# Gates spread by one product in the rounded format instead of one in full fp32

## The chip, the cores and the metric

The kernel runs on one core of a Trainium2 chip. The metric is the device time of one execution in microseconds; the median of the runs is compared. Five engines share the work: TensorE (PE; PEld its weight loads), VectorE (DVE), ScalarE (ACT), GpSimd (POOL) and SyncE (SP), each with an in-order queue of its own. Beside them the DMA engines move data.

## The reference, cut to what matters

Two transformer blocks run over 256 tokens of width 2048. The edit lies in the last part of the second one, a layer that picks 128 of 16384 experts for each token (8 heads, 16 each) and weighs them by a gate:

```
def peer_ffn(h, w_pq, sub_keys, u_tab, v_tab):
    ...
    expert = (e1 * N_KEYS + e2).reshape(T, PEER_HEADS * PEER_TOPK)
    gate = jax.nn.softmax(best, axis=-1).reshape(T, PEER_HEADS * PEER_TOPK).astype(h.dtype)
    ...
        u = jnp.take(u_tab, ec, axis=0)
        act = jax.nn.gelu(jnp.einsum('cd,ckd->ck', hc, u), approximate=False) * gc
        vv = jnp.take(v_tab, ec, axis=0)
        return jnp.einsum('ck,ckd->cd', act, vv)
```

An expert's number is e1 * 128 + e2, with e1 and e2 from 0 to 127.

## The kernel before

The kernel gathers no rows of `u_tab`. In `_peer` it computes Gelu(h u) for all 16384 experts and all 256 tokens, and multiplies the result by a matrix of gates that is zero where an expert wasn't picked. The result is `S_`, two tiles in SBUF: `sa` for the values 0 to 51 of e2 (SA = 52) and `sb` for 52 to 127, with e1 on the partitions and the tokens innermost. The next stage multiplies `S_` by `v_tab`.

The loop over i (64 passes) computes two values of e2 each. `_proj` streams 16 chunks of `u` through `_stream`: a DMA into `raw`, a ScalarE copy into the rounded format (`hi`, float32r, L252), a VectorE subtraction for the rest (`lo`, L255), 512 elements each, and per 128 columns three TensorE products of 256 moving columns (hi by hh, hi by hl, lo by hh) into `acc`. So each pass has 8 `hi`, 8 `lo` and 96 products. `hi` and `lo` have four buffers each. VectorE then scales `acc` into `gtmp` (L1564), ScalarE applies Gelu in one or two pieces (L1565, L1568), and `keep` sends the result to DRAM (`wide`) by DMAs that ScalarE issues (L1498). GpSimd multiplies the tokens whose gates are already there (L1570).

From i = G0 = 27 to 60 the loop also spreads gates, 256 tokens over 34 passes. `spread(g, e)` does four tokens (L1516 to L1539). For each token t the 128 picks lie on the partitions: `sel[:, 0]` is e1, `sel[:, 1]` is e2, `sel[:, 2]` the gate. A one-hot `oh1` (128 picks by 128 values of e1) and a one-hot `oh2` times the gate (128 picks by 128 values of e2) are built from `iota`, and one product of the two in full fp32 gives the token's matrix of gates in PSUM (`ps_g`). `oh1` is built in turn by VectorE and GpSimd (L1528), `oh2` by VectorE (L1529). For the e2 that are already computed, up to e, VectorE multiplies `S_` by `ps_g` (L1537); into the rest, where nothing stands yet, ScalarE copies `ps_g` (L1539).

The order of each engine's queue is set when the kernel is built: a scheduler interleaves the instructions of passes and spreads by its own cost model, and the queues then run strictly in that order, with semaphores between the engines. Pools limit how far ahead an engine may be: `gq` three buffers of one-hots (two tokens each), `psw` four banks for `ps_g`, `g1` one `gtmp`.

Of the kernel before, what the change touches and what calls it, by code (L numbers as in the profile page):

```python
# [10 lines left out]
F32 = mybir.dt.float32  # L11
# [1473 lines left out]
def _peer(k, I, O, hctx, pers, sa, tctx, t1, x3n, wide, rb):  # L1485
# [21 lines left out]
    with ExitStack() as sctx:  # L1507
        with ExitStack() as c:
            k.acc = c.enter_context(tc.tile_pool(name="accp", bufs=3, space=bass.MemoryType.PSUM, side="right"))
            k.psw = c.enter_context(tc.tile_pool(name="pswp", bufs=4, space=bass.MemoryType.PSUM))  # L1510
            t2 = tctx.enter_context(tc.tile_pool(name="rt2", bufs=2))
            route = _Route(k, I, rb, t1, t2)
            gq = None
            done = 0

            def spread(g, e):  # L1516


                ps = k.psw.tile([128, 4, 128], F32, name="ps_g", tag="psw")
                i0 = None  # L1520
                for j in range(4):
                    t = g * 4 + j
                    if j % 2 == 0:
                        a = gq.tile([128, 2, 128], F32, name="oh1")
                        b = gq.tile([128, 2, 128], F32, name="oh2")
                    aj, bj = a[:, j % 2], b[:, j % 2]
                    eng = nc.gpsimd if j % 2 else nc.vector
                    eng.tensor_scalar(aj, iota, sel[:, 0, t:t + 1], None, op0=OP.is_equal)  # L1528
                    nc.vector.tensor_scalar(bj, iota, sel[:, 1, t:t + 1], sel[:, 2, t:t + 1], op0=OP.is_equal, op1=OP.mult)  # L1529
                    i = _mm(k, ps[:, j], aj, bj, start=j == 0, stop=True)  # L1530
                    if j == 0:
                        i0 = i
                    else:
                        _after(k, i, i0)
                for s_, lo, hi in parts(0, e):
                    s_ = s_[:, :, g * 4:g * 4 + 4]
                    nc.vector.tensor_tensor(s_, s_, ps[:, :, lo:hi].rearrange("p t e -> p e t"), op=OP.mult)  # L1537
                for s_, lo, hi in parts(e, 128):
                    nc.scalar.activation(s_[:, :, g * 4:g * 4 + 4], ps[:, :, lo:hi].rearrange("p t e -> p e t"), AF.Copy)  # L1539


            for i in range(64):
                if i % 3 == 0 and i < 24:
                    route.head(i // 3)
                if i == 24:
                    route.finish(sel, picks)
                if i == SA // 2:
                    tctx.close()
                    sp = sctx.enter_context(tc.tile_pool(name="sb", bufs=1))
                    S_[1] = sp.tile([128, 128 - SA, 256], F32, name="sb")  # L1550
                    gq = c.enter_context(tc.tile_pool(name="gq", bufs=3))
                    g1 = c.enter_context(tc.tile_pool(name="gq1", bufs=1))
                    iota = g1.tile([128, 128], F32, name="iota")
                    nc.scalar.dma_start(iota, _cst(I, "iota"))
                ps = k.acc.tile([128, 2, 256], F32, name="acc")
                _proj(k, ps, I["u"][i], (0, KT), k.hh, k.hl)
                dst = next(parts(2 * i, 2 * i + 2))[0]
                if done == 0:
                    nc.vector.tensor_tensor(dst, ps, _bc2(rb), op=OP.mult)
                    nc.scalar.activation(dst, dst, AF.Gelu)  # L1560
                    keep(dst, i, 0, 256)
                else:
                    tmp = g1.tile([128, 2, 256], F32, name="gtmp")
                    nc.vector.tensor_tensor(tmp, ps, _bc2(rb), op=OP.mult)  # L1564
                    nc.scalar.activation(tmp[:, :, :done], tmp[:, :, :done], AF.Gelu)  # L1565
                    keep(tmp, i, 0, done)
                    if done < 256:
                        nc.scalar.activation(dst[:, :, done:], tmp[:, :, done:], AF.Gelu)  # L1568
                        keep(dst, i, done, 256)
                    nc.gpsimd.tensor_tensor(dst[:, :, :done], dst[:, :, :done], tmp[:, :, :done], op=OP.mult)  # L1570
                if i >= G0:
                    while done < 256 and done * (G1 - G0) < 256 * (i + 1 - G0):
                        spread(done // 4, 2 * i + 2)
                        done += 4
        hctx.close()

        with ExitStack() as c:
            pso = c.enter_context(tc.tile_pool(name="pso", bufs=1, space=bass.MemoryType.PSUM))
            v2 = c.enter_context(tc.tile_pool(name="v2", bufs=4, side="right"))
            k.raw2 = c.enter_context(tc.tile_pool(name="raw2", bufs=5, side="right"))  # L1580
            out = [[pso.tile([128, 512], F32, name=f"o{t}{q}") for q in range(4)] for t in range(2)]
            rows = c.enter_context(tc.tile_pool(name="vr", bufs=RB, side="right"))
            sums = _row_sums(k, picks, wide, rows, [out[t][3] for t in range(2)])
            taken = 0
            k.own, split = None, []

            def halves(e):


                src = S_[0][:, e] if e < SA else S_[1][:, e - SA]  # L1590
                ah = v2.tile([128, 256], F32R, name="ah")
                al = v2.tile([128, 256], F32R, name="al")
                nc.scalar.activation(ah, src, AF.Copy)
                i = nc.gpsimd.tensor_tensor(al, src, ah.bitcast(F32), op=OP.subtract)
                if k.own is not None:
                    k.tc.add_manual_dep(i.ins, k.own.ins.name, SYNC, reason="beside the sums")
                split.append((ah, al))

            halves(0)
            halves(1)  # L1600
            for e in range(128):
                ah, al = split.pop(0)
                for g, (vh, vl, _) in enumerate(_stream(k, I["v"][e], D - DS)):
                    for t in range(2):
                        ts = slice(t * 128, t * 128 + 128)
                        for n, (s_, m_) in enumerate(((ah, vh), (ah, vl), (al, vh))):
                            _mm(k, out[t][g], s_[:, ts], m_, start=e == 0 and n == 0, stop=e == 127 and n == 2)
                if e == 24:

                    xn = [S_[0][:, 8 * t:8 * t + 8].rearrange("p a b -> p (a b)").rearrange("p (a b) -> p a b", b=512) for t in range(2)]  # L1610
                    for t in range(2):
                        nc.scalar.dma_start(xn[t], x3n[t].rearrange("p (a b) -> p a b", b=512))
                while taken < 128 and taken * 122 < (e - 2) * 128:
                    next(sums, None)
                    taken += 1
                if e < 126:
                    halves(e + 2)
            for _ in sums:
                pass
            k.raw2 = None  # L1620
            sctx.close()
            fin = c.enter_context(tc.tile_pool(name="fin", bufs=1))
            nf = fin.tile([128, 4, 512], F32, name="nf")
            nc.scalar.dma_start(nf.rearrange("p a b -> p (a b)"), I["normf"].to_broadcast([128, D]))
            for t in range(2):
                ss = fin.tile([128, 4], F32, name=f"ss{t}")
                sq = fin.tile([128, 512], F32, name=f"fsq{t}")
                for q in range(4):
                    nc.vector.tensor_tensor(xn[t][:, q], xn[t][:, q], out[t][q], op=OP.add)
                    nc.scalar.activation(sq, xn[t][:, q], AF.Square, accum_out=ss[:, q:q + 1])  # L1630
                v = fin.tile([128, 1], F32, name=f"fv{t}")
                nc.vector.tensor_reduce(v, ss, axis=AX.X, op=OP.add)
                nc.vector.tensor_scalar(v, v, 1.0 / D, EPS, op0=OP.mult, op1=OP.add)
                r = _rsqrt(k, fin, v, 1, f"f{t}")
                for q in range(4):
                    nc.vector.scalar_tensor_tensor(xn[t][:, q], xn[t][:, q], r, nf[:, q], op0=OP.mult, op1=OP.mult)
                    (nc.sync if q % 2 else nc.scalar).dma_start(O["out"][t * 128:t * 128 + 128, q * 512:q * 512 + 512], xn[t][:, q])
# [146 lines left out]
```

## Time and profile before

| | |
|---|---|
| median of 3 runs | 3341.68 us (3337.93 to 3341.87) |
| profiled execution | 3346.09 us, span 3344.3 us |
| PE busy | 3243.8 us (97%) |
| PEld busy | 3051.6 us (91%) |
| DVE busy | 2480.0 us (74%) |
| ACT busy | 1570.2 us (47%) |
| POOL busy | 833.5 us (25%) |
| `ps_g` products | 512 instructions, from 2257.5 to 2737.5 us of the span |

The shares are averages over the whole span; for one stage a window has to be cut out. The chain of work that ended last is 86% TensorE. Busy time of an engine that isn't the bound costs nothing by itself; what counts is the wait that ends last.

### The profile page before, as it was taken

To read this page: it belongs to the slowest core of one execution; us is meant where nothing else is said; L and a number is where in the kernel's file an instruction comes from. 1 tells how busy PE (TensorE), PEld (TensorE's weight loads), DVE (VectorE), ACT (ScalarE), POOL (GpSimd) and SP (SyncE) were. 2 spreads that over 40 slices of the span, in tenths; PEclk is the share of its full clock that TensorE was granted. 3 is DMA by queue.
4 is the path that set the end of the run, shared out by engine and by line. 5 is a ranking of instruction groups with operands and counts; after the bars stand their busy time and mean duration, and the time that the engine had idled before them with its cause. 6 is when DMAs were issued, how large, how long until landed. Compare 5 with 4: busy or idle time off the path is not lost.

```text
span 3344.3 us, 65878 instructions
## 1 busy us (share of the span) xinstructions
PE 3243.8 (97%) x25018; PEld 3051.6 (91%) x25018; DVE 2480.0 (74%) x5503; ACT 1570.2 (47%) x2810; POOL 833.5 (25%) x1010
## 2 busy tenths in 40 slices
PE   8999899999999989999999899999999999999998
PEld 8999899999999979888869899999999997777776
DVE  8775587777754468887865687786777777999898
ACT  5444454444433345554454544444444444455554
POOL 3110100000000044444510000001222326666663
PEclk9999999999999989999999999999999999999999
DMA  5545455555555556444228766666656669999996
GB/s 196 162 160 171 145 169 180 188 179 188 179 187 183 180 178 208 151 132 137 91 88 261 242 208 193 203 187 196 180 174 182 180 185 319 355 347 345 345 344 237
DMA packets 240366, 680.47 MB, mean 203 GB/s; under 512 B 59184, under 2 KB 89776, under 8 KB 215856
## 3 DMA queue, kind: packets, MB, share of 16 engines
q1 hardware_dynamic: 168848, 560.53, 51.8%
q0 software_dynamic: 20480, 83.90, 7.1%
q10 hardware_dynamic: 50720, 31.82, 3.2%
q8 instruction: 196, 3.21, 0.4%
q14 instruction: 122, 1.00, 0.1%
HBM read 649.55 MB, written 60.16 MB: 212 GB/s over the span
## 4 chain that ended last, share of the span: by engine, by line
PE 86%; DVE 5%; DMA 4%; issue 2%; ACT 2%; POOL 1%; ACTq 0%; SPq 0%; DVEq 0%; POOLq 0%
PE acc L260 59%; PE o L260 15%; PE held L260 3%; PE ps_g L260 2%; PE R L260 1%; DMA raw<-in_w_out 1%; DVE lo L255 1%; ACT hi L252 1%; PE ps_S L260 1%; PE ps_p L260 1%; DMA x3n<-nat 0%; DVE hl L350 0%; PE ps_sc L260 0%; PE ps_m L260 0%; PE ps_go L260 0%
## 5 line engine op out<-in xcount | busy, mean ns | idle before, releaser
L252 ACT ACTIVATE hi<-raw 128x512 fp32r<-128x512 f32 (+1 forms) x1582 | 1146.4, 732 | 1335.3 <-PE acc L260 838.3
L255 DVE TENSOR_TENSOR lo<-raw,hi 128x512 fp32r<-128x512 f32 (+1 forms) x1492 | 1224.7, 835 | 631.3 <-ACT hi L252 588.1
L260 PE MATMUL acc<-hh,hi 128*128 128x256 f32 x4928 | 1403.5, 285 | 14.1 <-ACT hh L349 12.4
L260 PE MATMUL acc<-hh,lo 128*128 128x256 f32 x4928 | 1404.5, 286 | 9.9 <-DVE lo L255 9.1
L260 PE MATMUL acc<-hl,hi 128*128 128x256 f32 x4928 | 1398.1, 284 | 6.9 <-DVE hl L350 6.8
L260 PEld LDWEIGHTS acc<-hh,hi 128*128 128x128 f32 x4928 | 935.3, 190 | 17.6 <-ACT hh L349 13.2
L260 PEld LDWEIGHTS acc<-hl,hi 128*128 128x128 f32 x4928 | 935.4, 190 | 10.2 <-DVE hl L350 9.1
L260 PEld LDWEIGHTS acc<-hh,lo 128*128 128x128 f32 x4928 | 929.4, 189 | 15.1 <-DVE lo L255 12.0
L260 PE MATMUL o<-lo,ah 128*128 128x512 f32 x768 | 305.2, 398 | 2.5 <-issue 2.5
L260 PE MATMUL o<-hi,al 128*128 128x512 f32 x768 | 304.6, 397 | 0.9 <-issue 0.9
L1456 POOL DMA_INDIRECT vrow<-wide,prow x256 | 264.5, 1033 | 68.5 <-issue 42.7
L260 PE MATMUL o<-hi,ah 128*128 128x512 f32 x768 | 222.5, 399 | 8.5 <-ACT hi L252 5.8
L260 PE MATMUL acc<-gh,lo 128*128 128x256 f32 x704 | 199.2, 283 | 0.0
L260 PE MATMUL acc<-gl,hi 128*128 128x256 f32 x704 | 199.2, 283 | 0.0
L260 PE MATMUL acc<-gh,hi 128*128 128x256 f32 x704 | 199.2, 283 | 0.0
L260 PEld LDWEIGHTS o<-hi,ah 128*128 128x128 f32 x768 | 143.4, 189 | 48.7 <-ACT hi L252 10.7
L1528 POOL TENSOR_SCALAR oh<-iota,sel 128x128 f32<-128x128 f32 x128 | 95.4, 756 | 351.1 <-PE ps_g L260 321.1
L260 PEld LDWEIGHTS o<-lo,ah 128*128 128x128 f32 x768 | 145.0, 189 | 38.5 <-issue 2.9
L1478 DVE SCALAR_TENSOR_TENSOR o<-vrow,pval,o 128x512 f32<-128x512 f32 x254 | 179.1, 750 | 0.0
L260 PEld LDWEIGHTS o<-hi,al 128*128 128x128 f32 x768 | 145.0, 189 | 36.6 <-issue 1.3
L255 POOL TENSOR_TENSOR lo<-raw,hi 128x512 fp32r<-128x512 f32 (+1 forms) x90 | 135.1, 1503 | 170.4 <-ACT hi L252 154.3
L699 POOL MEMSET u<- 128x4 f32 x44 | 4.5, 103 | 653.7 <-DVE y L707 510.6
(474 smaller groups left out, 4366.8 us busy)
## 6 DMA issues: line engine op xcount, KB each, us to landing
raw<-in_u SPq DMA_DIRECT2D x256, 512.0 KB
raw<-in_w_up SPq DMA_DIRECT2D x85, 1024.0 KB
raw<-in_v SPq DMA_DIRECT2D x128, 512.0 KB
raw<-in_w_in SPq DMA_DIRECT2D x43, 1024.0 KB
raw<-in_w_dn SPq DMA_DIRECT2D x40, 1024.0 KB
wide<-in_vs SPq DMA_DIRECT2D x128, 256.0 KB
raw<-in_v SPq DMA_DIRECT2D x128, 256.0 KB
raw<-in_w_rkv SPq DMA_DIRECT2D x48, 512.0 KB
```

Of the source, the lines that this page charges most:

```text
L252: nc.scalar.activation(hi[:, :m], raw[:, a:a + m], AF.Copy)
L255: k.low = eng.tensor_tensor(lo[:, :m], raw[:, a:a + m], hi[:, :m].bitcast(F32), op=OP.subtract)
L260: return k.nc.tensor.matmul(out, lhsT, rhs, start=start, stop=stop, skip_group_check=True)
L699: nc.gpsimd.memset(u[:, :, 0:2], 0.0)
L1456: nc.gpsimd.indirect_dma_start(r, None, wide, bass.IndirectOffsetOnAxis(ap=picks.row[:, t, j:j + 1], axis=0), element_offset=128 * t)
L1478: i = nc.vector.scalar_tensor_tensor(acc[t], v, w, acc[t], op0=OP.mult, op1=OP.add)
L1528: eng.tensor_scalar(aj, iota, sel[:, 0, t:t + 1], None, op0=OP.is_equal)
```

## The change

`spread` now does two tokens instead of four. The gate is split once into a rounded part (`gate`, float32r) and the rest (written back into `sel[:, 2]`). For each token, `oh2` has two halves of 128 columns side by side, one times each part, all one-hots are in the rounded format, and one product of 256 moving columns gives both halves in PSUM. They have to be added afterwards: ScalarE copies the first half, VectorE adds the second. For the e2 already computed the sum goes into a new tile `gsum` (one for `sa`, one for `sb`) and VectorE multiplies `S_` by it in a further instruction; for the rest it goes straight into `S_`. GpSimd builds both `oh1` of a pair and one of the four halves of `oh2`; VectorE builds the other three. The pool `gq` has two buffers instead of three.

```diff
             def spread(g, e):
...
-                ps = k.psw.tile([128, 4, 128], F32, name="ps_g", tag="psw")
+                ps = k.psw.tile([128, 2, 2, 128], F32, name="ps_g", tag="psw")
+                a = gq.tile([128, 2, 128], F32R, name="oh1")
+                b = gq.tile([128, 2, 2, 128], F32R, name="oh2")
                 i0 = None
-                for j in range(4):
-                    t = g * 4 + j
-                    if j % 2 == 0:
-                        a = gq.tile([128, 2, 128], F32, name="oh1")
-                        b = gq.tile([128, 2, 128], F32, name="oh2")
-                    aj, bj = a[:, j % 2], b[:, j % 2]
-                    eng = nc.gpsimd if j % 2 else nc.vector
-                    eng.tensor_scalar(aj, iota, sel[:, 0, t:t + 1], None, op0=OP.is_equal)
-                    nc.vector.tensor_scalar(bj, iota, sel[:, 1, t:t + 1], sel[:, 2, t:t + 1], op0=OP.is_equal, op1=OP.mult)
-                    i = _mm(k, ps[:, j], aj, bj, start=j == 0, stop=True)
+                for j in range(2):
+                    t = g * 2 + j
+                    nc.gpsimd.tensor_scalar(a[:, j], iota, sel[:, 0, t:t + 1], None, op0=OP.is_equal)
+                    for n, w in enumerate((gate, sel[:, 2])):
+                        eng = nc.gpsimd if n and j else nc.vector
+                        eng.tensor_scalar(b[:, j, n], iota, sel[:, 1, t:t + 1], w[:, t:t + 1], op0=OP.is_equal, op1=OP.mult)
+                    i = _mm(k, ps[:, j].rearrange("p n e -> p (n e)"), a[:, j], b[:, j].rearrange("p n e -> p (n e)"),
+                            start=j == 0, stop=True)
...
-                for s_, lo, hi in parts(0, e):
-                    s_ = s_[:, :, g * 4:g * 4 + 4]
-                    nc.vector.tensor_tensor(s_, s_, ps[:, :, lo:hi].rearrange("p t e -> p e t"), op=OP.mult)
-                for s_, lo, hi in parts(e, 128):
-                    nc.scalar.activation(s_[:, :, g * 4:g * 4 + 4], ps[:, :, lo:hi].rearrange("p t e -> p e t"), AF.Copy)
+                for (s_, lo, hi), past in [(x, True) for x in parts(0, e)] + [(x, False) for x in parts(e, 128)]:
+                    s_ = s_[:, :, g * 2:g * 2 + 2]
+                    h, l = (ps[:, :, n, lo:hi].rearrange("p t e -> p e t") for n in range(2))
+                    if past:
+                        to = gq.tile([128, 128, 2], F32, name="gsum")[:, :hi - lo]
+                    else:
+                        to = s_
+                    nc.scalar.activation(to, h, AF.Copy)
+                    nc.vector.tensor_tensor(to, l, to, op=OP.add)
+                    if past:
+                        nc.vector.tensor_tensor(s_, s_, to, op=OP.mult)
...
-                    gq = c.enter_context(tc.tile_pool(name="gq", bufs=3))
+                    gq = c.enter_context(tc.tile_pool(name="gq", bufs=2))
...
+                    gate = g1.tile([128, 256], F32, name="gate")
+                    nc.scalar.activation(gate.bitcast(F32R), sel[:, 2], AF.Copy)
+                    nc.vector.tensor_tensor(sel[:, 2], sel[:, 2], gate, op=OP.subtract)
```

Because the scheduler lays the queues out anew, the order around the edit changes too. First ScalarE, around the two Gelus of one pass in the middle of the stage, before. A name's number is its buffer; what stands in brackets is what the instruction waits for.

```order
L252 ACTIVATE hi_29961<-raw_29959 128x512 [waits DMAHW4_49,DVE_49,PE_49]
L252 ACTIVATE hi_29977<-raw_29959 128x512 [waits DVE_49,PE_49]
L1565 ACTIVATE gtmp_29876<-gtmp_29876 128x2x76 [waits DMAHW0_49,DVE_49]
L1568 ACTIVATE sb_27763<-gtmp_29876 128x2x180
L1498 DMA wide_13452<-gtmp_29876 128x2x76 [waits Activation_49]
L1498 DMA wide_13452<-sb_27763 128x2x52 [waits Activation_49]
L1498 DMA wide_13452<-sb_27763 128x2x128 [waits DMAHW1_49]
L252 ACTIVATE hi_29995<-raw_29993 128x512 [waits DMAHW5_49,PE_49]
L252 ACTIVATE hi_30011<-raw_29993 128x512 [waits PE_49]
L1539 ACTIVATE sb_27763<-ps_g_29884 128x52x4 [waits DVE_49]
```

The same place after, at a pass a little later in the stage (L1574 and L1577 are the Gelus, L1542 the copies out of PSUM):

```order
L1542 ACTIVATE gsum_30982<-ps_g_30971 128x104 [waits DVE_49]
L1542 ACTIVATE sb_27763<-ps_g_30805 128x48x2 [waits DVE_49]
L252 ACTIVATE hi_31126<-raw_31124 128x512 [waits DMAHW2_49,PE_49,Activation_49]
L1574 ACTIVATE gtmp_30963<-gtmp_30963 128x2x98 [waits DMAHW5_49,DVE_49,Pool_49]
L1577 ACTIVATE sb_27763<-gtmp_30963 128x2x158
L1498 DMA wide_13452<-gtmp_30963 128x2x98 [waits Activation_49]
L1498 DMA wide_13452<-sb_27763 128x2x30 [waits DMAHW6_49,Activation_49]
L1498 DMA wide_13452<-sb_27763 128x2x128
L1542 ACTIVATE gsum_30986<-ps_g_30971 128x60 [waits DVE_49]
L1542 ACTIVATE gsum_31003<-ps_g_30992 128x104 [waits DVE_49]
L252 ACTIVATE hi_31142<-raw_31124 128x512 [waits PE_49]
```

Copies that wait for VectorE now stand both ahead of the Gelus and right behind the three DMA issues, ahead of the next `hi`.

VectorE, from `gtmp` of a pass on, before (L1537 multiplies `S_` by `ps_g`):

```order
L1564 TENSOR_TENSOR gtmp_29876<-acc_29739,rs_bcp_22242 128x512 [waits DMAHW0_49,PE_49,Pool_49]
L1537 TENSOR_TENSOR sa_20991<-sa_20991,ps_g_29884 128x52x4 [waits PE_49]
L1528 TENSOR_SCALAR oh1_30070<-iota_27770,sel_22346 128x128
L1529 TENSOR_SCALAR oh2_30071<-iota_27770,sel_22346 128x128 x2
L255 TENSOR_TENSOR lo_29978<-raw_29959,hi_29977 128x512 [waits Activation_49]
L1528 TENSOR_SCALAR oh1_30078<-iota_27770,sel_22346 128x128 [waits PE_49]
L1529 TENSOR_SCALAR oh2_30079<-iota_27770,sel_22346 128x128 x2
L1537 TENSOR_TENSOR sa_20991<-sa_20991,ps_g_29904 128x52x4 [waits PE_49]
```

And after, from `gtmp` of the pass shown above on (L1543 adds, L1545 multiplies):

```order
L1573 TENSOR_TENSOR gtmp_30963<-acc_30826,rs_bcp_22242 128x512 [waits DMAHW5_49,PE_49]
L255 TENSOR_TENSOR lo_31109<-raw_31090,hi_31108 128x512 [waits Activation_49]
L1545 TENSOR_TENSOR sb_27763<-sb_27763,gsum_30820 128x28x2 [waits DVE_49]
L1543 TENSOR_TENSOR gsum_30982<-ps_g_30971,gsum_30982 128x104 [waits Activation_49]
L1543 TENSOR_TENSOR sb_27763<-ps_g_30805,sb_27763 128x48x2 [waits Activation_49]
L255 TENSOR_TENSOR lo_31127<-raw_31124,hi_31126 128x512 [waits DMAHW2_49,PE_49,Activation_49]
L1545 TENSOR_TENSOR sa_20991<-sa_20991,gsum_30982 128x52x2 [waits DVE_49]
...
L1543 TENSOR_TENSOR gsum_30986<-ps_g_30971,gsum_30986 128x60 [waits Activation_49]
L1543 TENSOR_TENSOR gsum_31003<-ps_g_30992,gsum_31003 128x104 [waits Activation_49]
L1545 TENSOR_TENSOR sa_20991<-sa_20991,gsum_31003 128x52x2 [waits DVE_49]
L255 TENSOR_TENSOR lo_31143<-raw_31124,hi_31142 128x512 [waits PE_49,Activation_49]
```

Three two-operation one-hots stand where the row of dots is. Each multiplication waited for TensorE before; each addition waits for ScalarE now.

## Rows read from the trace of the kernel before

**Rows 1.** Busy time of each engine from 2350 to 2700 us, clock, DMA share.

```profile
core 0: us, PE busy (x) PEld busy (x) DVE busy (x) ACT busy (x) POOL busy (x), PEclk, DMA share, GB/s
2350.00:2700.00 350.00, 348.74 (x2936) 348.36 (x2935) 266.37 (x637) 161.51 (x314) 98.20 (x129) 1.00 0.61 180
```

**Rows 2.** Who waited for whom, same stretch: us in total, times, longest.

```profile
DVE lo L255 <- ACT hi L252: 59.8, 84, 1.5
...
PE acc L260 <- DVE lo L255: 1.3, 2, 0.9
```

**Rows 3.** TensorE in order of time: start us, us, instruction, count.

```profile
2506.77 0.28 PE L260 MATMUL acc<-hh,hi 128*128 128x256 f32 x1
2506.89 0.28 PE L260 MATMUL acc<-hl,hi 128*128 128x256 f32 x1
2507.00 1.05 PE L260 MATMUL ps_g<-oh,oh 128*128 128x128 f32 x8
2507.81 0.37 PE L260 MATMUL acc<-hh,lo 128*128 128x256 f32 x1
```

**Rows 4.** VectorE in order of time over one pass of the loop.

```profile
2551.99 0.69 DVE L1564 TENSOR_TENSOR gtmp<-acc,rs_bcp 128x512 f32<-128x512 f32 x1 [0.26 <-PE acc L260]
2552.60 0.30 DVE L1528 TENSOR_SCALAR oh<-iota,sel 128x128 f32<-128x128 f32 x1
2552.80 0.71 DVE L1529 TENSOR_SCALAR oh<-iota,sel 128x128 f32<-128x128 f32 x2
2553.42 0.68 DVE L255 TENSOR_TENSOR lo<-raw,hi 128x512 fp32r<-128x512 f32 x1
2554.03 0.36 DVE L1537 TENSOR_TENSOR sa<-sa,ps_g 128x208 f32<-128x208 f32 x1
2554.31 0.28 DVE L1528 TENSOR_SCALAR oh<-iota,sel 128x128 f32<-128x128 f32 x1
2554.50 1.10 DVE L1529 TENSOR_SCALAR oh<-iota,sel 128x128 f32<-128x128 f32 x2
...
2555.72 0.59 DVE L1529 TENSOR_SCALAR oh<-iota,sel 128x128 f32<-128x128 f32 x2
2556.24 0.36 DVE L1537 TENSOR_TENSOR sa<-sa,ps_g 128x208 f32<-128x208 f32 x1
...
2565.29 0.69 DVE L1564 TENSOR_TENSOR gtmp<-acc,rs_bcp 128x512 f32<-128x512 f32 x1 [0.26 <-PE acc L260]
```

**Rows 5.** ScalarE and its issues (ACTq) in order of time, two passes.

```profile
2552.72 0.45 ACT L1565 ACTIVATE gtmp<-gtmp 128x288 f32<-128x288 f32 x1 [0.27 <-DVE gtmp L1564]
...
2555.04 0.48 ACTq L1498 DMA_DIRECT2D wide<-sb  x1
2555.62 1.26 ACT L252 ACTIVATE hi<-raw 128x512 fp32r<-128x512 f32 x2 [2.18 <-PE acc L260]
...
2566.01 0.46 ACT L1565 ACTIVATE gtmp<-gtmp 128x304 f32<-128x304 f32 x1 [0.27 <-DVE gtmp L1564]
...
2567.43 0.70 ACTq L1498 DMA_DIRECT2D wide<-sb  x1
```

**Rows 6.** GpSimd: its one-hots as a group, then in order of time.

```profile
L1528 POOL TENSOR_SCALAR oh<-iota,sel 128x128 f32<-128x128 f32 x102 | 75.5, 751 | 251.5 <-PE ps_g L260 228.0 <-DVE lo L255 11.7 <-DVE sb L1537 9.1
...
2665.45 1.62 POOL L1528 TENSOR_SCALAR oh<-iota,sel 128x128 f32<-128x128 f32 x1 [4.20 <-PE ps_g L260]
2671.41 1.81 POOL L1528 TENSOR_SCALAR oh<-iota,sel 128x128 f32<-128x128 f32 x3 [4.34 <-PE ps_g L260]
2673.19 1.30 POOL L1570 TENSOR_TENSOR sb<-sb,gtmp 128x424 f32<-128x424 f32 x1
```

**Rows 7.** VectorE in order of time beside these GpSimd instructions.

```profile
2665.39 1.98 DVE L255 TENSOR_TENSOR lo<-raw,hi 128x512 fp32r<-128x512 f32 x3
...
2672.75 0.78 DVE L255 TENSOR_TENSOR lo<-raw,hi 128x512 fp32r<-128x512 f32 x1
2673.45 1.12 DVE L1529 TENSOR_SCALAR oh<-iota,sel 128x128 f32<-128x128 f32 x1
```

**Rows 8.** A ScalarE copy out of PSUM, by form, 2550 to 2600 us.

```profile
L1539 ACT ACTIVATE sb<-ps_g 128x112 f32<-128x112 f32 x1 | 0.3, 265 | 1.3 <-DVE sb L1537 1.3
```

More of the change, by code (lines that the diff above doesn't have):

```diff
@@ L1572, in _peer @@
                     while done < 256 and done * (G1 - G0) < 256 * (i + 1 - G0):
-                        spread(done // 4, 2 * i + 2)
-                        done += 4
+                        spread(done // 2, 2 * i + 2)
+                        done += 2
         hctx.close()
```

## The prediction

> **What bounds the kernel now.** I read the page's engine shares first, where TensorE leads. Since the edit lies in one stage, I then cut out the stretch in which gates are spread, and looked at who waits there and at the instructions in order of time. There TensorE is busy for 348.7 of 350 us at a granted clock of 1.00, VectorE for 266.4 and GpSimd for 98.2 [rows 1], and TensorE lost only 1.3 us to VectorE [rows 2]. So TensorE sets the pace here and VectorE has a quarter of its time free. The unit to count in is one pass of the loop over i, a "row". `gtmp` starts at 2551.99 and again at 2565.29 [rows 4], so a row takes 13.30 us; 34 rows (G0 to G1) share 256 tokens, 7.53 tokens or 3.76 pairs each.
>
> **What the change takes from TensorE.** Products of `acc` start 0.12 us apart (2506.77, 2506.89) [rows 3]; a row has 96, 11.52 us. The other 1.78 us are the gate products: each full fp32 one is two instructions in the trace, eight start in 0.81 us [rows 3], and with the change-over that makes 0.236 us a token. After, a token is one product of 256 moving columns in the rounded format, the very form of the `acc` products, so 0.12 us, 0.90 a row. TensorE then needs 12.42 us a row, 0.88 less; over 34 rows 29.9 us. That is all that can be won.
>
> **What it gives VectorE.** Spacing of starts, not durations, is what counts when it works without a break [rows 4]: `lo` 0.61 (2553.42 to 2554.03), `gtmp` 0.61, a one-operation one-hot 0.20, a two-operation one-hot 0.26 (two in 0.52 from 2555.72), a multiplication of 208 elements 0.28. From 512 elements in 0.60 and 208 in 0.28, a tensor_tensor costs 0.06 plus 1.05 ns per element. Before, a row is 8 `lo` and `gtmp` (5.4), 3.76 and 7.53 one-hots (0.75 and 1.92) and 3.76 multiplications (0.93): 9.0 us; 10.1 are measured (266.4 over 26.3 rows), the rest being collisions with GpSimd and ends before a wait. After, each pair of tokens brings three two-operation one-hots (0.78), three additions that together cover 256 elements (0.45) and two multiplications that cover 104 and on average 74 (0.31). A row: 5.4 + 2.9 + 1.7 + 1.15 = 11.15 us.
>
> To this comes GpSimd, which now builds three one-hots a pair instead of one, 11.3 a row. At 0.60 each when undisturbed (three in 1.81), and with the multiplication it has in each row, 0.9 ((98.2 - 75.5) / 26.3), it works for 7.7 us a row, more when disturbed [rows 1, 6]. Beside its multiplication a pair of one-hots on VectorE takes 1.10 instead of 0.59, beside its one-hots 0.71 [rows 4]. Once 0.5, and 0.06 for most of 11.3 one-hots, make 0.9 or so. **VectorE needs some 12.1 us of work a row, TensorE 12.42**: both nearly full, which only works if VectorE hardly waits.
>
> A rule of the Trainium skill speaks against this change (SBUF — State Buffer, "Who interferes with whom"): a VectorE instruction with two SBUF inputs and a GpSimd instruction that reads SBUF exclude each other for the whole instruction. The rows agree in part: a one-hot on VectorE took 1.12 beside GpSimd's multiplication and GpSimd's one-hot took 1.62 beside three `lo`, but three GpSimd one-hots took 1.81 while a `lo` ran in 0.78 [rows 6, 7]. By the rows I charge 0.9 us a row; by the rule it would be the third rival below.
>
> **Where VectorE waits.** This is the term that decides, and it comes from the order of ScalarE. Before, VectorE's multiplication read PSUM itself. Now each of the three parts of a pair goes PSUM, ScalarE copy, VectorE addition, and the copies stand in ScalarE's queue among `hi`, the two Gelus and the three DMA issues of `keep`. From the start of the first Gelu to the end of the last issue ScalarE is taken for 2.80 us (2552.72 to 2555.52) [rows 5]; in the next row it is 2.12 (2566.01 to 2568.13). Before, nothing but the next `hi` stands behind that block. After, copies do, and VectorE's addition, with `lo` queued behind it, waits for them.
>
> I walk the row of after whose order is printed above, from `gtmp` at 0, a copy at 0.26 [rows 8] and `hi` at 0.63 [rows 5]. `lo`, a short multiplication and an addition end at 1.50. The next addition needs a copy that itself waited for the multiplication just done: 0.3 lost. `lo_31127` needs `hi_31126`, which stands behind that copy, at 2.4: 0.45 lost. `lo`, a multiplication and three one-hots end at 3.95. The addition to `gsum_30986` needs the copy behind Gelus and issues, 2.4 + 2.8 + 0.26 = 5.45: 1.5 lost, 0.8 with the shorter block. `lo_31143` needs the second `hi` behind: 0.4 lost. Together 1.95 to 2.65 us. In the next row the Gelus come at 1.7, since no copy holds up the `hi` ahead of them, and the same steps lose 0.1 at a copy amid the issues, 0.65 at the first `hi` behind them and 0.15 at a later one, 0.9. I take 1.6 as the mean. TensorE hides a single stall, since four `hi` and `lo` buffers are up to three chunks of 1.44 us ahead, but not a sum that stays over its own need.
>
> **The sum.** VectorE 12.1 + 1.6 = 13.7 us a row against 13.30: 0.4 x 34 = 14 us more. The bounds: 0.9 lost a row and half the collisions give 12.5, 2.65 lost a row gives 14.75; that is -27 to +49 us. I take 13.7, between what the two walked rows give (13.0 and up to 14.75). Preparing `gate` costs one pass of 256 elements each on ScalarE and VectorE, under 0.5 us once [rows 4, 8], beside products. The two one-hot buffers instead of three cost nothing: GpSimd needs some 2.3 to 3 us for a pair and pairs come every 3.5; if it needed over 3.5, it would be the bound. The profiled execution took 3346.1 us (span 3344.3), 4.4 over the median of the runs; differences carry over, so I set them on 3341.7: **3356 us**.
>
> **Rivals.**
> - *TensorE stays the bound.* If the copies come early enough, or the buffers swallow the stalls, a row takes 12.42 to 13.1: 7 to 30 us less, about 3323. For it: TensorE waited only 1.3 us while VectorE waited 59.8 us for `hi` [rows 2], so waits there are mostly slack, and a VectorE that lags finds more copies done. Against: 12.1 of 12.42 leaves no slack to use up. Chance 0.27.
> - *It cancels.* A row of 13.1 to 13.5, within 7 us of before, 3342. Chance 0.20.
> - *GpSimd and VectorE exclude each other.* If every one-hot, `lo` and multiplication from SBUF of VectorE (2.9 + 4.9 + 1.15) ran alone against GpSimd's 7.7, a row would take 16.6, +112 us, 3454. It decides from the point where one GpSimd one-hot delays VectorE by over 0.15 us (11.15 + 0.5 + 11.3 x 0.15 is 13.3), even with no wait; the `lo` beside three of them was held up by 0.1 in all (0.70 to the next start) [rows 7]. With long stalls in every row (over 14.3) as the milder form. Chance 0.08 together.
> - *The products don't get cheaper.* Then TensorE keeps 13.3; the `acc` rows of the same form exclude it.
>
> **How the numbers follow.** The forecast, 13.5 to 14.3 us a row or +7 to +34 us, has 0.45. About 0.2%, 7 us, is what a measurement of this kernel can tell from no change. Faster takes the first rival, 0.27; same 0.20; slower the forecast and the third, 0.53. The range leaves about a tenth out at each end: 3320 (a row of 12.66) to 3382 (a row of 14.5). The forecast's own is 3349 to 3376.
>
> **What would show it.** In the stage's windows TensorE should fall from 99.6% to some 91%, VectorE rise to about 88%, GpSimd to over 55%. The waits should list TensorE for `lo`, and VectorE's additions (L1543) for ScalarE's copies (L1542), over 1 us a row; a row should be near 13.7. Gate products should start 0.12 apart. If rows are near 12.5 and TensorE waits for nothing, the stalls were slack and I am wrong on the wait. If VectorE's one-hots and `lo` themselves grow well over 0.4 and 0.8, I am wrong on the collisions.

## The result and the profile after

The changed kernel takes 3311.87 us (median of 6, 3309.78 to 3319.35), the kernel before 3341.77 us (median of 6, 3337.93 to 3345.34). The ratio is 0.9915, with a 95% interval of 0.9902 to 0.9928: 29.9 us less at the medians. The forecast, 14 us more, was wrong, and so was the sign. What happened is the first rival, "TensorE stays the bound". The profiled execution has a span of 3313.4 us.

The stretch 2350 to 2675 us, which lies in the same stage as [rows 1] and has its columns (TensorE, weight loads, VectorE, ScalarE, GpSimd, granted clock):

```profile
2350.00:2675.00 325.00, 323.38 (x2701) 322.97 (x2700) 311.44 (x999) 192.71 (x547) 287.54 (x317) 1.00 0.65 190
```

TensorE is still busy for 99.5%, as before, but now beside a VectorE that is busy for 95.8% (76% before) and a GpSimd that is busy for 88% (28% before). A row, one pass of the loop over i, is read over the whole stage: `gtmp` starts at 2309.3 and, 35 rows later, at 2743.6, so 12.41 us a row. In the kernel before, 2313.0 to 2772.4 gives 13.13 (my single pass of [rows 4] had 13.30). The stage's end, where the first product of `o` starts, moved from 2773.2 to 2744.4: 28.8 of the 29.9 us.

Who waits for whom in that stretch (us in total, times, longest), to be held against [rows 2]:

```profile
ACT hi L252 <- PE acc L260: 51.7, 83, 1.9
...
DVE sb L1545 <- DMA wide<-sb: 7.2, 5, 3.4
...
DVE lo L255 <- ACT hi L252: 4.3, 12, 0.8
...
PE acc L260 <- DVE lo L255: 1.6, 2, 1.2
...
DVE gsum L1543 <- ACT gsum L1542: 0.3, 1, 0.3
```

VectorE's wait for `hi` fell from 59.8 us (in the 350 us of [rows 2]) to 4.3. The wait on which my forecast stood, an addition (L1543) for a ScalarE copy (L1542), appears once, with 0.3 us. ScalarE waits most for TensorE to free a buffer, so the engine that sets the pace has not changed.

The gate products of a pair, in order of time on TensorE, to be held against [rows 3]:

```profile
2521.71 0.28 PE L260 MATMUL acc<-hh,lo 128*128 128x256 f32 x1
2521.82 0.40 PE L260 MATMUL ps_g<-oh,oh 128*128 128x256 f32 x2
2522.06 0.28 PE L260 MATMUL acc<-hl,hi 128*128 128x256 f32 x1
```

The next product starts 0.24 us after the first of these two (2521.82 to 2522.06), so one takes 0.12, as priced.

The same stretch by groups (busy us, mean ns of one, idle time before):

```profile
L1525 POOL TENSOR_SCALAR oh<-iota,sel 128x128 fp32r<-128x128 f32 x194 | 154.8, 808 | 37.5 <-PE ps_g L260 26.5 <-DVE sb L1543 4.3 <-DVE lo L255 4.2
L1528 POOL TENSOR_SCALAR oh<-iota,sel 128x128 fp32r<-128x128 f32 x97 | 112.3, 1158 | 0.0
...
L255 DVE TENSOR_TENSOR lo<-raw,hi 128x512 fp32r<-128x512 f32 x209 | 146.2, 703 | 5.1 <-ACT hi L252 4.3 <-ACT sb L1542 0.2
L1528 DVE TENSOR_SCALAR oh<-iota,sel,gate 128x128 fp32r<-128x128 f32 x192 | 69.5, 363 | 0.6 <-PE ps_g L260 0.2
```

GpSimd's one-hots take 0.81 us (one operation, L1525) and 1.16 us (two operations, L1528) where I had reckoned 0.60 for either, while VectorE's `lo` at 0.70 and two-operation one-hots at 0.36 are hardly longer than the undisturbed ones of [rows 4] (0.68, and 0.33 from the pair of 0.59 with its spacing of 0.26).

### The profile page after: what moved, and what is told of

It reads as the page before. It is cut to its first block, busy times and chain, and to the rows that moved or that the text cites. A ratio compares the mean times of both kernels' runs of the same rounds, so it can differ in the third digit from the quotient of the medians.

```text
span 3313.4 us, 66459 instructions
## 1 busy us (share of the span) xinstructions
PE 3217.2 (97%) x24762; PEld 3024.0 (91%) x24762; DVE 2556.5 (77%) x6016; ACT 1614.8 (49%) x3131; POOL 1079.8 (33%) x1266
## 4 chain that ended last, share of the span: by engine, by line
PE 83%; DVE 8%; DMA 5%; ACT 2%; issue 1%; POOL 1%; ACTq 0%; SPq 0%; DVEq 0%
PE acc L260 57%; PE o L260 15%; PE held L260 3%; DVE lo L255 2%; DMA raw<-in_w_out 1%; PE R L260 1%; PE ps_g L260 1%; ACT hi L252 1%; DVE hl L350 1%; PE ps_S L260 1%; DVE ltmp L1040 1%; DMA x3n<-nat 1%; PE ps_p L260 0%; DMA dst<-s 0%; PE ps_sc L260 0%
## 5 line engine op out<-in xcount | busy, mean ns | idle before, releaser
L260 PE MATMUL acc<-hh,lo 128*128 128x256 f32 x4928 | 1401.9, 285 | 11.4 <-DVE lo L255 10.4
L260 PEld LDWEIGHTS acc<-hh,hi 128*128 128x128 f32 x4928 | 934.8, 190 | 16.5 <-ACT hh L349 12.3
L1525 POOL TENSOR_SCALAR oh<-iota,sel 128x128 fp32r<-128x128 f32 x256 | 203.0, 803 | 93.2 <-PE ps_g L260 79.7
```

What stands on the lines that cost most here:

```text
L260: return k.nc.tensor.matmul(out, lhsT, rhs, start=start, stop=stop, skip_group_check=True)
L1525: nc.gpsimd.tensor_scalar(a[:, j], iota, sel[:, 0, t:t + 1], None, op0=OP.is_equal)
```

## The experiments

Two theories stood against each other for the missing 44 us. The first: VectorE works as much as I priced, but its waits for ScalarE aren't there, because a VectorE that lags finds the copies done. The rival: the work itself was priced too high, and the kernel has room to spare. Unless it says otherwise, an edit is made to the changed kernel, and ratios are to the kernel before, measured beside it.

### Every copy out of PSUM made twice

```
                     nc.scalar.activation(to, h, AF.Copy)
+                    nc.scalar.activation(to, h, AF.Copy)
```

> Changed kernel with each ScalarE copy out of PSUM made twice: ScalarE's work grows by some 2.3 us a row and each chain from product to addition by 0.15 to 0.25 us. Theory 1 (waits for copies are slack): within 5 us of the changed kernel, 3308 to 3317. The prediction's step (VectorE's waits for copies add to its work): the waits grow by about 1 us a row, 20 to 40 us slower than the changed kernel, 3332 to 3352.

3315.3 us, ratio 0.9917 [0.9900, 0.9935]. Its stretch from 2350 to 2675 us, and then TensorE's longest wait in the stage:

```profile
2350.00:2675.00 325.00, 325.00 (x2716) 324.83 (x2715) 308.26 (x972) 237.47 (x812) 270.92 (x304) 1.00 0.66 190
```

```profile
PE o L260 <- DVE gtmp L1574: 9.5, 1, 9.5
```

VectorE's waits in the stretch, for `hi` and for a copy:

```profile
DVE lo L255 <- ACT hi L252: 10.4, 24, 0.9
...
DVE gsum L1544 <- ACT gsum L1543: 0.5, 2, 0.3
```

ScalarE works 45 us more in the stretch (237.47 against 192.71) and TensorE doesn't notice there; at the end of the stage it waits once for a VectorE that has fallen behind. The wait for a copy stays at next to nothing (0.5 us, against 0.3 in the changed kernel); it is `hi`, behind the copies, that comes somewhat later (10.4 us of waits instead of 4.3). The time can't be told from that of the changed kernel: by the ratios and their intervals the copies made twice cost at most some 8 us, and the 20 to 40 us that the prediction's step asked for are excluded. I had charged VectorE's waits for the copies with 1.6 us a row, 54 us in all.

### VectorE builds all four gated one-hots, or half of GpSimd's share

```
-                        eng = nc.gpsimd if n and j else nc.vector
+                        eng = nc.vector                                          (x4_dve4)
+                        eng = nc.gpsimd if n and j and g % 2 else nc.vector      (x5_half)
```

> Changed kernel with all four halves of the second one-hot on VectorE, none on GpSimd: VectorE's work grows by 3.76 x 0.26 = 1.0 us a row less some 0.3 for fewer collisions, 12.5 to 12.9 against TensorE's 12.42. Theory 1 with VectorE's work as the next bound: 3 to 16 us slower than the changed kernel, 3315 to 3328. If GpSimd (88% busy) was the engine at the edge: same or faster, 3308 to 3312.

> Changed kernel with the fourth half of the second one-hot on VectorE for every other pair: half the step of x4_dve4. VectorE's work 11.9 + 0.5 - 0.1 = 12.3 us a row against TensorE's 12.42. If the pace turns where VectorE's work passes TensorE's need: within 6 us of the changed kernel, 3308 to 3318. If VectorE needs spare time for its waits, so that the edge lies below 12.42: half of x4_dve4's loss or so, 3320 to 3335.

All four: 3350.48 us, ratio 1.0023 [1.0013, 1.0033]. Half: 3322.93 us, ratio 0.9946 [0.9928, 0.9964]. First two stretches of the kernel with all four, and what TensorE waited for from 2540 to 2790 us:

```profile
2350.00:2550.00 200.00, 200.00 (x1672) 200.00 (x1672) 190.73 (x618) 115.52 (x318) 85.76 (x118) 1.00 0.65 191
2550.00:2780.00 230.00, 201.38 (x1599) 198.87 (x1597) 212.80 (x674) 118.93 (x342) 111.13 (x136) 0.95 0.58 171
```

```profile
PE acc L260 <- DVE gtmp L1573: 18.7, 8, 4.8
PE o L260 <- DVE gtmp L1573: 8.9, 1, 8.9
```

For 200 us nothing is to be seen: TensorE is busy without a break while VectorE falls behind. Then the backlog is paid: TensorE waits for `gtmp` to free an `acc` buffer, and its granted clock is 0.95 over that stretch instead of 1.00. From 2584 to 2588 us, for instance, TensorE is busy for 0.24 us; from 2588 to 2590 its granted clock is 0.53, most of it at the lower of its two levels (1.2 of 2.4 GHz), and from 2592 on 1.00 again. With half the share most of VectorE's backlog is paid in one piece, at the stage's end:

```profile
2350.00:2675.00 325.00, 325.00 (x2716) 324.88 (x2716) 314.26 (x1008) 190.75 (x533) 211.22 (x251) 1.00 0.65 191
```

```profile
PE o L260 <- DVE gtmp L1573: 12.7, 1, 12.7
PE acc L260 <- DVE gtmp L1573: 4.3, 3, 2.6
```

In the changed kernel the wait of `o` is 0.9 us, and `acc` never waits for `gtmp`. A gated one-hot a pair is 3.76 x 0.26 = 0.98 us a row, 33 us over 34 rows, and VectorE's busy time in the stage did rise by 32.4 us (443.8 from 2309 to 2781.3, against 411.4 from 2309.3 to 2743.6 in the changed kernel). By the ratios it cost 36 us (1.0023 against 0.9915). On TensorE's side the 36 consist of its waits for `gtmp`, 27.6 us, and of the lower clock, by an estimate from its row another 0.05 x 230 = 11.5; the changed kernel has some waits of its own, so the two make a little more than 36. Half of the one-hots, priced at 17 us, cost 10 by the ratios, with an interval of some 4 to 17.

Both expectations need an answer. The first was missed: 3315 to 3328 were expected, since I counted on fewer collisions and on a pace that turns only where VectorE's work passes 12.42 us a row. Of the second the later branch came true: the edge lies below 12.42. The expectation puts that down to the time that VectorE needs for the waits it has left; it is idle for 10.7 us of the 325 with half the share, but no run takes those waits away. So VectorE's work counts nearly in full from where the changed kernel stands; how much of it was still free there, by the ratios 7 us or none, these runs don't settle. My price of the work was right, and the rival theory of room to spare falls.

### GpSimd builds both low parts

```
-                        eng = nc.gpsimd if n and j else nc.vector
+                        eng = nc.gpsimd if n else nc.vector
```

> Changed kernel with both halves for the rest of the gate on GpSimd: it builds four one-hots a pair, VectorE two. VectorE's work falls to some 10.9 us a row. GpSimd's, by its fastest (0.60 and 0.79), is 10.5 + 1.1 = 11.6 a row, by its means in the changed kernel (0.80 and 1.15) 14.7 + 1.1 = 15.8. If the means come from collisions with a full VectorE and fall with its load: 12.42 to 13 a row, 3308 to 3332. If GpSimd's durations stay: 14 to 15.8, 3365 to 3427.

3359.8 us, ratio 1.0052 [1.0032, 1.0072]. The stretch, and TensorE's waits in it:

```profile
2350.00:2675.00 325.00, 309.01 (x2434) 298.75 (x2433) 264.72 (x815) 175.84 (x495) 322.48 (x368) 0.98 0.60 173
```

```profile
PE acc L260 <- DVE lo L255: 8.1, 5, 2.6
PE ps_g L260 <- POOL oh L1528: 7.0, 19, 0.7
```

GpSimd is now busy for 99%, and a row is 13.70 us (2309.6 to 2789.0 over 35): GpSimd can't give gates any faster. That lies between the two ranges expected, since its one-hots became shorter with less on VectorE, 0.79 and 1.02 us instead of 0.81 and 1.16, but not as short as undisturbed ones. The 8.1 us for `lo` are a loss beside that, in which VectorE's waits for a DMA (24.0 us for `wide<-sb`, taken up in the next experiment) have a part that wasn't separated. The changed kernel stands between two edges: one one-hot of a pair more on either engine, and the whole gain is gone.

### Less work: no additions, and the rounded format alone

The first leaves the second half of `ps_g` unread: no additions, and a copy only for the open part. The second is the kernel before with nothing but the one-hots' format changed.

```
-                    nc.scalar.activation(to, h, AF.Copy)
-                    nc.vector.tensor_tensor(to, l, to, op=OP.add)
...
+                    nc.vector.tensor_tensor(s_, s_, ps[:, :, 0, lo:hi].rearrange("p t e -> p e t"), op=OP.mult)
```

> Changed kernel without the second half: products stay 256 columns, but the half in PSUM that belongs to the rest of the gate is not read; VectorE multiplies by the first half straight out of PSUM and ScalarE copies it only where nothing stands yet. So two of three ScalarE copies, all additions and the low part of the gate are left out. VectorE's work falls from some 11.9 us a row to about 9.9 and GpSimd's stays. Theory 1 (TensorE sets the pace, VectorE's and ScalarE's new work is hidden): as the changed kernel within 4 us, 3308 to 3316. Theory 2 (VectorE at 96% busy, or its waits for copies, still hold TensorE up): faster than the changed kernel by more than 6 us.

```
-                        a = gq.tile([128, 2, 128], F32, name="oh1")
-                        b = gq.tile([128, 2, 128], F32, name="oh2")
+                        a = gq.tile([128, 2, 128], F32R, name="oh1")
+                        b = gq.tile([128, 2, 128], F32R, name="oh2")
```

> The kernel before with its one-hots in the rounded format and nothing else: one product of 128 columns per token, gate rounded (its low part is left out), no additions. Theory 1: TensorE needs 0.06 to 0.10 us a token instead of 0.12, a row of 12.0 to 12.3, 4 to 15 us faster than the changed kernel, 3297 to 3308. If a 128-column product costs the same 0.12 because the weight load sets its spacing, 3312 again. Theory 2: faster than that, since VectorE's load is gone.

Without additions: 3332.11 us, ratio 0.9964 [0.9951, 0.9977]. One rounded product: 3334.04 us, ratio 0.9972 [0.9961, 0.9982]. Both do less than the changed kernel and both are slower, by 16 and 19 us if the ratios are compared. This I hadn't expected, and no theory had a place for it. The waits from 2300 to 2750 us say where to look (each trace is one execution, that of one rounded product the fastest of its ten, 3324.79 us). First without additions:

```profile
DVE sb L1537 <- DMA wide<-sb: 47.0, 24, 3.9
...
PE acc L260 <- DVE lo L255: 6.7, 11, 1.7
PE ps_g L260 <- ACT sb L1539: 4.4, 6, 1.4
```

and with one rounded product:

```profile
DVE sb L1537 <- DMA wide<-sb: 63.7, 26, 6.2
...
PE acc L260 <- DVE lo L255: 11.9, 11, 3.4
```

`keep` stores the open part of a row out of `sb` by DMA, and the multiplication of that part of `sb` must wait until the store has read it. A pass of the kernel without additions, all engines, in order of time (in brackets the idle time before, and its releaser):

```profile
2650.15 0.27 PE L260 MATMUL acc<-hl,hi 128*128 128x256 f32 x1
2650.49 0.65 DVE L1537 TENSOR_TENSOR sb<-sb,ps_g 128x116 f32<-128x116 f32 x3 [3.10 <-DMA wide<-sb]
2650.80 0.57 ACT L1539 ACTIVATE sb<-ps_g 128x36 f32<-128x36 f32 x3 [3.02 <-DVE sb L1537]
2651.05 0.68 DVE L255 TENSOR_TENSOR lo<-raw,hi 128x512 fp32r<-128x512 f32 x1
...
2651.14 0.47 PE L260 MATMUL ps_g<-oh,oh 128*128 128x256 f32 x2 [0.72 <-ACT sb L1539]
...
2651.79 0.39 PE L260 MATMUL acc<-hh,lo 128*128 128x256 f32 x1 [0.17 <-DVE lo L255]
```

VectorE stands for 3.1 us in front of the multiplication, with `lo` queued behind it, and ScalarE's copies out of `ps_g` wait for that multiplication too. TensorE uses up what it had; then it waits 0.72 us for such a copy to free a bank and 0.17 for `lo`. The chain of waits of that kernel holds the store in pass after pass (start, us, what):

```profile
2645.23 5.23 DMA wide<-sb
...
2659.35 5.35 DMA wide<-sb
```

The same wait is 23.6 us in the kernel before, where TensorE needs longer for a row and loses only 2.3 us to `lo` over that stretch, and 7.2 us in the changed kernel. That VectorE comes to the multiplication later there, since it has three additions a pair to do while the store is under way, is a likely reason that no run tests.

### The same four kernels with the store moved off `sb`

If that is the cause, it must go once `keep` reads only `gtmp`. The edit is made to the two kernels just told, to the changed kernel and to the one before:

```
-                    nc.scalar.activation(tmp[:, :, :done], tmp[:, :, :done], AF.Gelu)
-                    keep(tmp, i, 0, done)
                     if done < 256:
                         nc.scalar.activation(dst[:, :, done:], tmp[:, :, done:], AF.Gelu)
-                        keep(dst, i, done, 256)
+                    nc.scalar.activation(tmp, tmp, AF.Gelu)
+                    keep(tmp, i, 0, 256)
```

> x1_noadd (additions and the low half of the gate left out), but keep sends all 256 tokens from gtmp: ScalarE applies Gelu to the open tokens twice, once into sb and once in place, so no DMA reads sb any more while gates are spread and VectorE's multiplications need not wait for one. If x1_noadd was slower than the changed kernel because VectorE reached those multiplications before the DMA had landed (47 us of waits there, with lo queued behind): as the changed kernel or better, 3305 to 3316. If the cause is another part of the new order: still 3325 to 3335.

> x2_one (one 128-column product per token, gate rounded, its low part left out), with the same sending from gtmp. A 128-column product starts 0.10 us after the last in x2_one, so TensorE needs 11.52 + 7.53 x 0.12 or less, 12.3 to 12.4 a row. If the DMA wait was the cause (64 us of waits in x2_one): 3305 to 3314. If not: 3325 to 3335.

> Changed kernel with the same sending from gtmp. Its VectorE waited only 7 us for that DMA and TensorE 2 us for lo, so by the theory that TensorE sets the pace: within 5 us of the changed kernel, 3307 to 3316; ScalarE has 0.3 us a row more to do. If the waits for the DMA still cost it: 5 to 10 us faster.

> Kernel before with the same sending from gtmp. Its TensorE lost 2.3 us in the stage and VectorE has a quarter of its time free, so the 24 us that VectorE waited for the DMA were slack: within 6 us of before, 3335 to 3347. If those waits held it back too: 10 us faster or more.

| kernel | as it was | store from `gtmp` |
| --- | --- | --- |
| before | 1 | 1.0000 [0.9989, 1.0012] |
| changed | 0.9915 [0.9902, 0.9928] | 0.9918 [0.9902, 0.9935] |
| without additions | 0.9964 [0.9951, 0.9977] | 0.9914 [0.9895, 0.9932] |
| one rounded product | 0.9972 [0.9961, 0.9982] | 0.9909 [0.9890, 0.9928] |

The cause is shown: the wait for the store is gone from both kernels' lists, both come down to the changed kernel's time, and the other two, where the wait cost TensorE next to nothing, don't move. The stretch from 2350 to 2675 us, without additions and with one rounded product, both with the store from `gtmp`:

```profile
2350.00:2675.00 325.00, 324.75 (x2715) 324.54 (x2714) 278.76 (x726) 173.89 (x360) 279.61 (x320) 1.00 0.62 192
```

```profile
2350.00:2675.00 325.00, 325.00 (x2728) 325.00 (x2728) 259.08 (x634) 167.15 (x312) 102.54 (x125) 1.00 0.63 192
```

TensorE is busy without a break in both, with a VectorE at 86% and 80%. All four kernels at 0.991 to 0.992 stand at the same bound, TensorE's own work, and no relief of VectorE takes them below it. No version tried is clearly faster than the changed kernel: 3309.01 us for one rounded product with the store moved is within its interval.

## Why the prediction was wrong, step by step

**What bounds the kernel now** held: TensorE, with VectorE a quarter free.

**What the change takes from TensorE** held for the row after: 12.42 us were worked out and 12.41 measured. That 29.9 us were named as all that can be won and 29.9 were won is partly luck. The row before is 13.13 over the stage and not the 13.30 of my one pass, so a full fp32 product cost 0.21 us a token and not 0.236, and the rows give 0.72 x 34 = 24.5 us. The rest came elsewhere: 3.7 us lie ahead of the stage's first `gtmp` (2313.0 before, 2309.3 after), and 1.3 of these even ahead of the loop's first scaling of `acc` (1896.1 and 1894.8), where nothing of the edit lies.

**What it gives VectorE** held: 12.1 us a row worked out, 311.44 / (325 / 12.41) = 11.9 measured, and the one-hots added in x4_dve4 cost VectorE what the spacing of starts said. GpSimd was mis-sized: 7.7 us a row "more when disturbed", against 287.54 / 26.2 = 11.0. A part of that is no collision: every third of its one-hots now has two operations, which take 0.80 undisturbed (shortest in x1_noadd 0.79), and I had reckoned 0.60 for all. I had put 0.9 us of collisions on VectorE, of which by the same sum some 0.75 were there (11.9 less 11.15), and none in numbers on GpSimd, where they were over 2 us. That did no harm to the time only because 11.0 is still below 12.4.

**Where VectorE waits** is the step that failed. I predicted 1.6 us a row and added it to the work. In the stretch VectorE is idle for 13.6 us in all (325 less 311.44), 0.52 a row, and for the copies 0.3 us in 26 rows. The walk set ScalarE and VectorE off together at `gtmp`, with no work in hand. In the trace VectorE lags. Here it is around one pass's `gtmp`, first VectorE:

```profile
2522.64 0.68 DVE L1573 TENSOR_TENSOR gtmp<-acc,rs_bcp 128x512 f32<-128x512 f32 x1
...
2524.06 0.68 DVE L255 TENSOR_TENSOR lo<-raw,hi 128x512 fp32r<-128x512 f32 x1
...
2524.99 0.71 DVE L255 TENSOR_TENSOR lo<-raw,hi 128x512 fp32r<-128x512 f32 x1
2525.62 0.24 DVE L1545 TENSOR_TENSOR sb<-sb,gsum 128x76 f32<-128x76 f32 x1
...
2526.59 0.22 DVE L1543 TENSOR_TENSOR sb<-ps_g,sb 128x76 f32<-128x76 f32 x1
2526.74 0.25 DVE L1543 TENSOR_TENSOR gsum<-ps_g,gsum 128x104 f32<-128x104 f32 x1
```

and ScalarE with its DMA issues (ACTq):

```profile
2521.97 0.63 ACT L252 ACTIVATE hi<-raw 128x512 fp32r<-128x512 f32 x1 [0.90 <-PE acc L260]
...
2523.66 0.63 ACT L252 ACTIVATE hi<-raw 128x512 fp32r<-128x512 f32 x1 [0.81 <-DMA raw<-in_u]
2524.20 0.42 ACT L1574 ACTIVATE gtmp<-gtmp 128x272 f32<-128x272 f32 x1
...
2524.64 0.92 ACTq L1498 DMA_DIRECT2D wide<-gtmp  x2
2525.61 0.26 ACT L1542 ACTIVATE sb<-ps_g 128x76 f32<-128x76 f32 x1 [0.70 <-DVE gsum L1543]
2525.64 0.46 ACTq L1498 DMA_DIRECT2D wide<-sb  x1
2526.14 0.26 ACT L1542 ACTIVATE gsum<-ps_g 128x104 f32<-128x104 f32 x1 [0.27 <-ACT sb L1542]
```

The `lo` of 2524.06 can't have used the `hi` of 2523.66, which ends at 2524.29; it used an earlier one, so VectorE is a chunk behind ScalarE. The block of Gelus and issues lasts from 2524.20 to 2526.10, 1.90 us where I had taken 2.80 and 2.12; that it is shorter isn't the reason, since it lasts 2.73 in the next pass (2534.97 to 2537.70). The copy behind it ends at 2526.40; VectorE, busy with what stands ahead in its queue (two `lo`, two multiplications, two additions and three one-hots from 2524.06 on), comes to its addition at 2526.74. None of the three stalls that I had walked through the block is there, nor one in the next pass.

Adding waits walked from an empty queue to the work was the mistake in the method. An engine that lacks time falls behind its supplier, and by falling behind it stops waiting. In the changed kernel a row takes the larger of TensorE's 12.42 and VectorE's 12.1, and not 12.1 + 1.6. The larger of the two is a floor, not a law: in x5_half VectorE's work, some 12.3 by price, is still below 12.42, and its row is (2755.3 - 2305.4) / 35 = 12.85. Copies made twice (x3_act2) show that VectorE's wait for a copy isn't there to be lengthened; the one-hots moved (x4_dve4, x5_half) show that work on VectorE is what counts.

**The rivals.** The first named the reason itself, "a VectorE that lags finds more copies done", and gave 7 to 30 us less; I gave it 0.27. The argument against it, that 12.1 of 12.42 leaves no slack, was no argument against this kernel: the little that VectorE still waits, 0.52 us a row, fits beside its 11.9. It is right about what lies beyond, as x5_half shows. The range ended at 3320, a row of 12.66, although 12.42 had been worked out as the least a row can take; with that as its lower end (3311.8) it would just have reached the time.

The third rival, that VectorE and GpSimd exclude each other, is not borne out. `lo` (209 at 0.60) and the multiplications from SBUF (190 at 0.17, by the 0.06 and 1.05 ns) would need 158 us of the stretch alone; GpSimd's one-hots undisturbed (194 at 0.60; 97 at 0.80, one that ran by itself in x1_noadd) and its multiplication (0.9 x 26.2) would need 218. Together, 376 us don't fit one after the other into 325, even with VectorE's one-hots left out. They disturb each other, mostly at GpSimd's expense. The Trainium skill's rule (SBUF — State Buffer, "Who interferes with whom"), an exclusive lock for the whole instruction, would have made a row longer than it is; the trace disagrees in that, and agrees that the two engines slow each other.

**What would show it** named the outcome: rows near 12.5 with TensorE waiting for nothing would mean that the stalls were slack. That is what the trace shows.

## What to carry to other kernels

Don't add a walked engine's waits to its work while buffers let it lag: begin with the larger of the engines' work per step, and ask of each wait whether it remains once the waiting engine is late. With the two engines' work within a few per cent of each other (x5_half), the larger alone was 0.4 us a row too little. When an engine has a few per cent of its time left, price an added instruction in full, and read the place where a backlog is paid at the end of the stage, since the stretch in the middle looks perfect. When work is taken away and a kernel gets slower, look for an instruction that now comes too early for a DMA that reads its target, and send the DMA from another buffer.

## What the runs showed of the hardware

- A rounded product of 128 columns is nearly as dear as one of 256. With one rounded product per token, six start in 0.62 us, 0.103 each (2341.63 to 2342.25 below), against 0.120 for 256 columns. The second half, the low part of the gate, therefore costs TensorE only some 0.017 us a token.

```profile
2341.63 0.78 PE L260 MATMUL ps_g<-oh,oh 128*128 128x128 f32 x6
2342.25 0.33 PE L260 MATMUL acc<-hh,hi 128*128 128x256 f32 x1
```

- ScalarE computes while its DMA issues are in hand. In the changed kernel a `hi` starts at 2535.72 beside two issues that last until 2537.14; I had counted the issues as time in which nothing else runs. What stands behind an issue seems to wait for it all the same: in the pass shown further up, a copy starts at 2525.61, 0.05 us after the issues of 2524.64 end, and another at 2526.14, 0.04 after the next issue ends.

```profile
2535.72 0.64 ACT L252 ACTIVATE hi<-raw 128x512 fp32r<-128x512 f32 x1
2535.74 1.40 ACTq L1498 DMA_DIRECT2D wide<-gtmp  x2
```
